# Seven pairs of converted weight blocks and three raw buffers in place of six and four

## The chip, the cores and the metric

The kernel runs on one core of one Trainium2 chip. The metric is the device time of one execution in microseconds (us); the median of the runs shown counts.

## The reference

One sequence of 256 tokens of 1024 features runs through two stacks of two layers each, all in float32. A layer of the first stack is a half-weighted SwiGLU block, a mixer and another half-weighted SwiGLU block:

```
x = x + 0.5 * swiglu(rms_norm(x, norm_ffn1[l]), ...)      # d_ff 2816
x = x + hybrid_mixer(rms_norm(x, norm_mix[l]), w_in[l], ...)
x = x + 0.5 * swiglu(rms_norm(x, norm_ffn2[l]), ...)
```

The hybrid mixer has dilated window attention (12 heads in three groups) and stick-breaking attention (4 heads), each behind a sigmoid gate, and a projection out. A layer of the second stack is a mixer with four branches (compressed, selected and window attention; a sliding window attention with sinks; a 31-tap depthwise convolution with a layer norm; windowed mean pooling), each gated by `sigmoid(h @ w_gate)`, followed by a block `w_down(gelu(conv3(h @ w_up_gate)) * conv3(h @ w_up_value))`, each with a norm behind it. A last RMS norm closes the first stack. All weight matrices together are some 366 MB and are read once.

## The kernel before

All activations stay on the chip; only weights stream in. Every weight product is done as three float32r products: both factors are split into a rounded part and the rest (`h` and `l`, or `wh` and `wl`), and `h*wh + h*wl + l*wh` is summed in PSUM (`mm3`, lines 191 to 194, and the two transposed forms `lin_T` and `lin_T2`, lines 202 to 228).

A weight block of 128 partitions x 1024 elements (512 KB; some are smaller) passes four engines in `chunk` (lines 112 to 120). SyncE issues its load into a tile of the pool `rawp` (line 115); ScalarE rounds it into a tile `wh` (line 118); VectorE subtracts, `wl = raw - wh` (line 119); TensorE uses the pair. The pool `wp` has `bufs` tiles of each of the two tags `wh` and `wl`, so `bufs` is the number of converted pairs. A load can be issued when the tile that it overwrites was read for the last time, by the subtraction; a rounding can start when the last matmul has read the pair that it overwrites. Each tile of a full block has 4 KB in each partition.

The loops over the blocks differ in how long they hold a pair. `lin` (line 196) runs all eight k for the first 128 tokens and then for the second, so a pair is given back in the second pass. `lin_T`, `lin_T2` and `kouter` (line 249) use a block up and give it back, except that `kouter` with `late` holds the last four blocks for the second half of the tokens, so that TensorE has work while the norms behind the first half run. In the second mixer (`mixer2`, line 660) some blocks are used up faster: `compress` (line 766) needs eight matmuls of 256 columns for a block, where the others need 12 of 512, and one projection of 280 columns has blocks of 280 KB.

The kernel is one unrolled program of 30596 instructions. Which engine runs what is written in the source; the order on each engine and all semaphores are laid down when the program is built, by a planner that goes by the order in the source, its own estimate of the durations, and the buffers that are free. `behind` (line 277) sets a few orders by hand. Each engine then runs its queue strictly in that order. The convolution of the second mixer (lines 951 to 956) is 120 VectorE instructions per layer that depend on little else; its result is wanted at the end of the mixer. `stat` (line 57) hands out tiles of 8 columns for maxima, sums and norms.

Of the kernel before, what the change touches and what calls it, by code (L numbers as in the profile page):

```python
# [8 lines left out]
F32 = mybir.dt.float32  # L9
F32R = mybir.dt.float32r  # L10
BF16 = mybir.dt.bfloat16
AF = mybir.ActivationFunctionType
OP = mybir.AluOpType
AX = mybir.AxisListType

P = 128
# [9 lines left out]
def body(tc, ctx, I, C, out, upto=99):  # L26
    nc = tc.nc
    V, S, G = nc.vector, nc.scalar, nc.gpsimd

    rawp = ctx.enter_context(tc.tile_pool(name="rawp", bufs=4))  # L30
    wp = ctx.enter_context(tc.tile_pool(name="wp", bufs=6))
    act = ctx.enter_context(tc.tile_pool(name="act", bufs=1))
    gp = ctx.enter_context(tc.tile_pool(name="gp", bufs=1))
    st = ctx.enter_context(tc.tile_pool(name="st", bufs=1))
# [6 lines left out]
    def nm(s):  # L41
        uid[0] += 1
        return f"{s}{uid[0]}"
# [11 lines left out]
        return psum.tile([P, 512], F32, tag="aux", name=nm("aux"))  # L55

    def stat(cols=1):
        return st.tile([P, 8], F32, tag="st", name=nm("st"), bufs=48)[:, :cols]

    pending, pows, early = [], [], []  # L60

# [89 lines left out]

    def split(src, hi, lo, scale=None):
        if scale is None:
            S.activation(hi, src, AF.Copy)
            V.tensor_sub(lo, src, hi.bitcast(F32))  # L155
        else:
            S.activation(hi, src, AF.Copy, scale=scale)  # L157
            V.scalar_tensor_tensor(lo, src, scale, hi.bitcast(F32), op0=OP.mult, op1=OP.subtract)  # L158

    def transposed(srcs):  # L160
        p = aux_ps()
# [13 lines left out]
    def split_T(tag, srcs, scale=None):  # L175

        xt = XT()
        if len(srcs) == 1:
            n = srcs[0].shape[-1]
            b = big(tag, "hl", F32R)  # L180
            hi, lo = b[:, :n], b[:, 512:512 + n]
            split(transposed(blocks(srcs[0], n // P)), hi, lo, scale)
            xt.add(hi, lo, n // P)
        else:
            bh, bl = big(tag, "hi", F32R), big(tag, "lo", F32R)
            for s, hi, lo in zip(srcs, halves(bh), halves(bl)):
                split(transposed(blocks(s)), hi, lo, scale)
                xt.add(hi, lo)
        return xt
# [91 lines left out]
    def square(src):  # L281

        junk = unit("junk", BF16, 1024)[:, :src.shape[-1]]
        m = stat()
        S.activation(junk, src, AF.Square, scale=1.0 / 32.0, accum_out=m)
        return m

    def rstd_of(parts):

        r, r2 = stat(), stat()  # L290
        V.tensor_scalar(r, parts[0], parts[1], EPS, op0=OP.add, op1=OP.add)
        pows.append(G.tensor_tensor(r2, r, half, op=OP.pow))
        return r2
# [24 lines left out]
    class Halves:  # L318
# [5 lines left out]
        def put(self, t, b, src):  # L324
            hi, lo = (halves(x)[b] for x in self.bufs[t])
            split(transposed(blocks(src)), hi, lo, self.scale)
            self.xts[t].add(hi, lo)
# [91 lines left out]
    def attend1(qkn, vs):  # L419
# [3 lines left out]
        for t in range(2):  # L423
# [27 lines left out]
            def scores(js):  # L451

                r = [([], stat(4), stat(4)) for _ in js]
                for gi, gs in enumerate(groups):
                    n = len(gs) * nk * P
                    pss = [aux_ps()[:, :n] for _ in js]
                    for gg in gs:
                        for kt in range(nk):
                            c0 = ((gg - gs[0]) * nk + kt) * P
                            for ps, j in zip(pss, js):  # L460
                                h = gg * 4 + j
                                nc.tensor.matmul(ps[:, c0:c0 + P], qk(h, False, t), qk(h, True, kt),
                                                 start=(gg == gs[0] and kt == 0), stop=(gg == gs[-1] and kt == nk - 1))
                    for ps, (ps_l, mx, sm) in zip(pss, r):
                        e = unit("e")[:, :n]
                        masked(e, ps, dilm[t][:, gs[0]:gs[-1] + 1, :].rearrange("p g k -> p (g k)"), mx[:, gi:gi + 1])
                        ps_l.append(e)
                return r
# [780 lines left out]
```

## Time and profile before

| | |
|---|---|
| median of 3 runs | 2100.12 us (2099.17 to 2103.72) |
| the profiled execution's own time | 2096.72 us |
| its span, first to last instruction | 2094.9 us |
| TensorE matmul busy, share of the span | 98% |
| TensorE weight load busy | 83% |
| VectorE busy | 75% |
| ScalarE busy | 57% |
| mean granted TensorE clock | 0.999 |
| read from HBM | 366.10 MB, 175 GB/s over the span |

The profile is that of one execution. PE is TensorE's matmul, PEld its weight load, DVE VectorE, ACT ScalarE, SP SyncE; a q behind a name is the queue that an engine issues from. A busy time is the union of the records, and matmul records overlap: the records of 512 columns are about 0.39 us long and start 0.23 us apart. Idle time is put down to the work whose end released the waiting instruction.

### The profile page before, as it was taken

How to read it: one execution, taken by the hardware profiler on the slowest of the kernel's cores; microseconds unless marked ns; L12 is line 12 of the kernel's file. 1: busy time of each engine (PE TensorE's matmuls, PEld its weight loads, DVE VectorE, ACT ScalarE, POOL GpSimd, SP SyncE). 2: the span in 40 equal slices, each digit the busy share in tenths (PEclk: the TensorE clock that was granted, in tenths of full speed). 3: DMA queues.
4: the chain of work that ended last, by engine and by line, in shares of the span. 5: the costliest groups of instructions: out<-in, count | busy, mean ns of one | idle time of the engine just before them, and what ended most of it. 6: DMA issues, size and time to landing. Idle time of an engine off the chain costs nothing.

```text
span 2094.9 us, 30596 instructions
## 1 busy us (share of the span) xinstructions
PE 2059.3 (98%) x11428; PEld 1737.9 (83%) x11428; DVE 1574.7 (75%) x2696; ACT 1185.2 (57%) x1905; POOL 27.6 (1%) x51
## 2 busy tenths in 40 slices
PE   8999999999999999999999999999999999999998
PEld 7888877888888887788887877779987877788997
DVE  7865466886688556678757999778867899877883
ACT  6555565554555455565545665456655565557652
POOL 0000000000000000000000000000000000000000
PEclk9999999999999999999999999999999999999999
DMA  9665535666666654466666733556665744365653
GB/s 268 194 191 173 191 120 165 187 190 192 181 191 190 186 177 150 142 176 188 191 190 183 229 121 121 175 164 194 183 193 176 219 149 142 101 202 172 181 189 112
DMA packets 248102, 368.70 MB, mean 176 GB/s; under 512 B 14608, under 2 KB 123536, under 8 KB 247952
## 3 DMA queue, kind: packets, MB, share of 16 engines
q1 hardware_dynamic: 247088, 366.17, 57.1%
q8 instruction: 90, 1.47, 0.3%
q0 software_dynamic: 576, 0.46, 0.1%
q14 instruction: 60, 0.49, 0.1%
q10 hardware_dynamic: 288, 0.11, 0.0%
HBM read 366.10 MB, written 1.05 MB: 175 GB/s over the span
## 4 chain that ended last, share of the span: by engine, by line
PE 87%; DVE 7%; ACT 2%; DMA 2%; issue 1%; POOL 0%; DVEq 0%; POOLq 0%; SPq 0%; ACTq 0%
PE lin L194 16%; PE lin L193 16%; PE lin L192 15%; PE lin L226 15%; PE lin L227 8%; PE lin L214 3%; PE lin L213 3%; PE lin L212 3%; PE aux L163 3%; DVE wl L119 2%; DVE cy L955 1%; ACT wh L118 1%; DVE e L275 1%; PE aux L650 1%; PE aux L597 1%
## 5 line engine op out<-in xcount | busy, mean ns | idle before, releaser
L119 DVE TENSOR_TENSOR wl<-raw,wh 128x1024 fp32r<-128x1024 f32 (+2 forms) x689 | 834.9, 1216 | 377.1 <-ACT wh L118 370.6
L118 ACT ACTIVATE wh<-raw 128x1024 fp32r<-128x1024 f32 (+2 forms) x689 | 721.9, 1052 | 509.6 <-PE lin L194 273.7
L226 PE MATMUL lin<-x,wh 128*128 128x512 f32 x1408 | 490.5, 394 | 0.0
L227 PE MATMUL lin<-x,wl 128*128 128x256 f32 x1408 | 392.2, 279 | 0.4 <-DVE wl L119 0.4
L194 PE MATMUL lin<-wh,x 128*128 128x512 f32 (+2 forms) x896 | 347.0, 388 | 2.7 <-DVE x L158 2.6
L193 PE MATMUL lin<-wl,x 128*128 128x512 f32 (+2 forms) x896 | 347.5, 388 | 1.9 <-DVE wl L119 1.9
L192 PE MATMUL lin<-wh,x 128*128 128x512 f32 (+2 forms) x896 | 347.4, 388 | 0.8 <-ACT x L157 0.8
L226 PEld LDWEIGHTS lin<-x,wh 128*128 128x128 f32 x1408 | 263.9, 187 | 59.5 <-DVE x L158 0.3
L227 PEld LDWEIGHTS lin<-x,wl 128*128 128x128 f32 x1408 | 265.5, 189 | 1.1 <-DVE wl L119 0.8
L192 PEld LDWEIGHTS lin<-wh,x 128*128 128x128 f32 x896 | 168.4, 188 | 39.4 <-issue 5.2
L194 PEld LDWEIGHTS lin<-wh,x 128*128 128x128 f32 x896 | 168.4, 188 | 38.9 <-DVE x L158 7.3
L193 PEld LDWEIGHTS lin<-wl,x 128*128 128x128 f32 x896 | 168.5, 188 | 35.0 <-DVE wl L119 3.0
L194 PE MATMUL lin<-wh,lo 128*128 128x512 f32 x480 | 188.2, 392 | 0.5 <-DVE lo L155 0.5
L192 PE MATMUL lin<-wh,hi 128*128 128x512 f32 x480 | 187.6, 391 | 0.0
L193 PE MATMUL lin<-wl,hi 128*128 128x512 f32 x480 | 187.0, 390 | 0.0
L213 PE MATMUL lin<-x,wh 128*128 128x256 f32 x576 | 163.2, 283 | 0.0
L214 PE MATMUL lin<-x,wl 128*128 128x256 f32 x576 | 163.0, 283 | 0.0
L212 PE MATMUL lin<-x,wh 128*128 128x256 f32 x576 | 163.0, 283 | 0.0
L213 PEld LDWEIGHTS lin<-x,wh 128*128 128x128 f32 x576 | 110.6, 192 | 0.1
L212 PEld LDWEIGHTS lin<-x,wh 128*128 128x128 f32 x576 | 110.6, 192 | 0.1
L214 PEld LDWEIGHTS lin<-x,wl 128*128 128x128 f32 x576 | 110.6, 192 | 0.0
L194 PEld LDWEIGHTS lin<-wh,lo 128*128 128x128 f32 x480 | 90.1, 188 | 19.6 <-DVE lo L155 1.3
(300 smaller groups left out, 2609.6 us busy)
## 6 DMA issues: line engine op xcount, KB each, us to landing
raw<-in_ffn_w_up_dram SPq DMA_DIRECT2D x168, 512.0 KB, 3.8
raw<-in_ffn_w_down_dram SPq DMA_DIRECT2D x132, 512.0 KB, 3.7
raw<-in_w_in_dram SPq DMA_DIRECT2D x132, 512.0 KB, 4.0
raw<-in_ffn_w_gate_dram SPq DMA_DIRECT2D x87, 512.0 KB, 3.8
raw<-in_w_gate_dram SPq DMA_DIRECT2D x64, 512.0 KB, 4.3
raw<-in_w_branch_dram SPq DMA_DIRECT2D x32, 512.0 KB, 3.5
raw<-in_w_out_dram SPq DMA_DIRECT2D x16, 512.0 KB, 4.5
raw<-in_nsa_cmp_w_dram SPq DMA_DIRECT2D x16, 512.0 KB, 4.4
```

The lines of the kernel that those rows point to most:

```text
L118: S.activation(wh, raw, AF.Copy)
L119: V.tensor_sub(wl, raw, wh.bitcast(F32))
L163: nc.tensor.transpose(p[:, i * P:(i + 1) * P], s, ident)
L192: nc.tensor.matmul(ps, xt.h[k], w[0], start=start, stop=False)
L193: nc.tensor.matmul(ps, xt.h[k], w[1], start=False, stop=False)
L194: nc.tensor.matmul(ps, xt.l[k], w[0], start=False, stop=stop)
L212: nc.tensor.matmul(o, wh, xh, start=k == 0 and i % 2 == 0, stop=False)
L213: nc.tensor.matmul(o, wh, xl, start=False, stop=False)
L214: nc.tensor.matmul(o, wl, xh, start=False, stop=k == 7 and i % 2 == 1)
L226: nc.tensor.matmul(o, wh, x, start=k == 0, stop=False)
L227: nc.tensor.matmul(o[:, :T], wl, x[:, :T], start=False, stop=k == 7)
L275: V.tensor_tensor_reduce(out, ps, mask, 1.0, NEG, OP.add, OP.max, mx)
```

## The change

The pool of raw blocks has three tiles in place of four, the pool of converted blocks seven pairs in place of six. The statistics tiles go from 48 to 40, 256 bytes of each partition less, beside 8 KB more for the pair and 4 KB less for the raw tile. `split` gives back the instructions that it issues; nobody uses them.

```diff
-    rawp = ctx.enter_context(tc.tile_pool(name="rawp", bufs=4))
-    wp = ctx.enter_context(tc.tile_pool(name="wp", bufs=6))
+    rawp = ctx.enter_context(tc.tile_pool(name="rawp", bufs=3))
+    wp = ctx.enter_context(tc.tile_pool(name="wp", bufs=7))
...
-        return st.tile([P, 8], F32, tag="st", name=nm("st"), bufs=48)[:, :cols]
+        return st.tile([P, 8], F32, tag="st", name=nm("st"), bufs=40)[:, :cols]
...
     def split(src, hi, lo, scale=None):
         if scale is None:
-            S.activation(hi, src, AF.Copy)
-            V.tensor_sub(lo, src, hi.bitcast(F32))
-        else:
-            S.activation(hi, src, AF.Copy, scale=scale)
-            V.scalar_tensor_tensor(lo, src, scale, hi.bitcast(F32), op0=OP.mult, op1=OP.subtract)
+            return S.activation(hi, src, AF.Copy), V.tensor_sub(lo, src, hi.bitcast(F32))
+        return (S.activation(hi, src, AF.Copy, scale=scale),
+                V.scalar_tensor_tensor(lo, src, scale, hi.bitcast(F32), op0=OP.mult, op1=OP.subtract))
```

## Rows read from the trace of the kernel before

**Rows 1.** Page, busy time: engine, us, share of the span, instructions.
```profile
PE 2059.3 (98%) x11428; PEld 1737.9 (83%) x11428; DVE 1574.7 (75%) x2696; ACT 1185.2 (57%) x1905; POOL 27.6 (1%) x51
```

**Rows 2.** Table of stages: length; busy us, instructions by engine; clock; DMA share; GB/s.
```profile
20.00:165.00 145.00, 145.00 (x797) 125.96 (x796) 112.43 (x146) 82.57 (x122) 0.00 (x0) 1.00 0.70 214
...
250.00:300.00 50.00, 48.06 (x314) 38.58 (x314) 33.36 (x86) 29.16 (x53) 0.00 (x0) 1.00 0.40 127
...
800.00:850.00 50.00, 47.68 (x318) 37.88 (x316) 36.02 (x95) 32.60 (x62) 0.00 (x0) 1.00 0.34 105
...
1150.00:1330.00 180.00, 175.41 (x1007) 140.46 (x1008) 171.41 (x429) 106.24 (x218) 2.30 (x3) 1.00 0.51 157
1645.00:1830.00 185.00, 179.14 (x1014) 142.73 (x1014) 173.04 (x431) 106.18 (x218) 2.08 (x2) 0.99 0.49 153
```

**Rows 3.** Waits of weight loads: who for whom; total us, times, longest us.
```profile
PEld lin L194 <- DVE x L158: 7.3, 12, 1.1
...
PEld aux L163 <- DVE kd L572: 4.0, 2, 2.3
...
PEld lin L193 <- DVE wl L119: 3.0, 5, 1.0
...
PEld lin L227 <- DVE wl L119: 0.8, 1, 0.8
...
PEld lin L192 <- ACT wh L118: 0.6, 3, 0.2
```

**Rows 4.** Groups by form: line, engine, tiles, count; busy us, mean ns; idle before.
```profile
L119 DVE TENSOR_TENSOR wl<-raw,wh 128x1024 fp32r<-128x1024 f32 x679 | 827.7, 1223 | 373.0 <-ACT wh L118 366.6
L118 ACT ACTIVATE wh<-raw 128x1024 fp32r<-128x1024 f32 x679 | 715.3, 1058 | 503.5 <-PE lin L194 273.7 <-issue 156.9 <-PE lin L213 41.9
```

**Rows 5.** Timelines of ScalarE, VectorE, SyncE near 550 us: start, length, what, idle before.
```profile
549.35 1.06 ACT L118 ACTIVATE wh<-raw 128x1024 fp32r<-128x1024 f32 x1 [1.66 <-PE lin L194]
552.07 1.06 ACT L118 ACTIVATE wh<-raw 128x1024 fp32r<-128x1024 f32 x1 [1.66 <-PE lin L194]
...
550.44 1.23 DVE L119 TENSOR_TENSOR wl<-raw,wh 128x1024 fp32r<-128x1024 f32 x1 [1.50 <-ACT wh L118]
...
551.69 0.37 SPq L115 DMA_DIRECT2D raw<-in_ffn_w_up_dram  x1
```

**Rows 6.** Timelines of TensorE and VectorE in the second mixer's attention.
```profile
1271.36 0.50 PE L192 MATMUL lin<-wh,x 128*128 128x512 f32 x1
...
1272.80 0.50 PE L193 MATMUL lin<-wl,x 128*128 128x512 f32 x1
...
1271.44 1.22 DVE L119 TENSOR_TENSOR wl<-raw,wh 128x1024 fp32r<-128x1024 f32 x1
```

**Rows 7.** DMA issues from 1150 to 1175 us: count, KB each, median us to landing.
```profile
raw<-in_w_in_dram SPq DMA_DIRECT2D x7, 512.0 KB, 4.3
raw<-in_w_in_dram SPq DMA_DIRECT2D x4, 280.0 KB, 3.2
```

**Rows 8.** SyncE's timeline; line 118 from 1144 to 1186 us (ns min/median/max; idle until).
```profile
1157.65 18.02 SPq L115 DMA_DIRECT2D raw<-in_w_in_dram  x12
...
L118 ACT ACTIVATE wh<-raw x21: 672/1057/1065, 1144.5 to 1184.7; 128x1024 fp32r<-128x1024 f32 x17, 128x560 fp32r<-128x560 f32 x4
...
  DMA raw<-in_w_in_dram: 3.4, 6
```

**Rows 9.** Timelines of SyncE and VectorE at the start.
```profile
13.58 2.23 SPq L115 DMA_DIRECT2D raw<-in_ffn_w_gate_dram  x2
...
14.18 1.22 DVE L119 TENSOR_TENSOR wl<-raw,wh 128x1024 fp32r<-128x1024 f32 x1
```

**Rows 10.** Table of stages, the 5 us in which the granted clock fell.
```profile
1820.00:1825.00 5.00, 4.10 (x22) 3.45 (x22) 1.77 (x3) 1.06 (x1) 1.56 (x1) 0.81 0.25 57
```

## The prediction

> **What bounds the kernel now.** I read the busy times of the engines first: TensorE is busy for 2059.3 us of a span of 2094.9 us, so at most 35.6 us of the span can be won by feeding it better [rows 1]. VectorE has 75% over the whole. The table of stages then says where the idle time lies. In long stretches of plain weight products TensorE is busy for all of it (145.00 of 145 us from 20 to 165 us), and there no buffer can help. It idles in the first mixer's attention (1.94 us from 250 to 300 us, 2.32 us in the second layer's counterpart) and in the two passes of the second mixer (4.6 of 180 us and 5.9 of 185 us). In those two passes VectorE is busy for 171.4 of 180 and 173.0 of 185 us, so there are two nearly full engines that wait for each other [rows 2].
>
> The Trainium skill (Perfetto Trace Analysis, Identifying the Most-Contended Engine) says that busy matmuls are a poor measure of headroom and that the busy share of the weight loads is a good one. Weight loads are busy for 83% here, so by that rule 17% of the span, some 357 us, would be open. In the stretch in which TensorE never waits the weight loads have 125.96 of 145 us, 87%, so this trace doesn't bear the rule out: 83% is close to full [rows 1, 2].
>
> The third view is what the weight loads waited for. Waits for a converted block are small: 3.0 us for wl before line 193, 0.8 us for wl before line 227, 0.6 us for wh before line 192, 4.4 us in nine places of the whole run. Waits for the two rows that head the list, activations being turned (7.3 us) and a rope result (4.0 us), have nothing to do with the weights [rows 3].
>
> **The weight pipeline.** A block of 512 KB is loaded by SyncE into a raw buffer, ScalarE rounds it to wh in 1.06 us, VectorE takes the difference to wl in 1.22 us; 679 full blocks [rows 4]. In a steady stretch wh starts every 2.72 us, each time after ScalarE waited 1.6 us for a matmul to give back a pair; the load that follows is issued when wl is done, the difference that ends at 551.67 us being followed by a load at 551.69 us [rows 5]. So in the steady state the six pairs are full, four raw blocks wait landed behind them, and TensorE sets the pace.
>
> **The change, part by part.**
>
> *One pair more.* No instruction is added. In the steady state each block is converted one release, 2.72 us, earlier, and TensorE gains nothing, for it never waits there. What can go are waits for wl and wh: of the 4.4 us the 0.8 us of line 227 belongs to the first blocks, where no pair is short, which leaves 3.6 us. The longest of them is about 1 us, shorter than the 2.72 us of lead, so each would go if nothing took its place. But they lie in the passes in which VectorE has 95% and 94% [rows 2, 3]. There an earlier difference is another VectorE instruction later. An example: at 1271.36 TensorE starts one weight product, and the next starts only at 1272.80, right behind a difference that VectorE ran from 1271.44 to 1272.66 [rows 6]. With a pair more this difference would have been done before; what VectorE does in its place is a step of the rope that ends 1.2 us earlier, or one of the convolution. Bounds: 0 if all is given back, 3.6 us if nothing is; half, 1.8 us, because one of the two neighbours is filler (the convolution) and the other is a chain.
>
> *One raw buffer less.* The load of block n+3, not n+4, now waits for the difference of block n. A raw buffer's round is 4.3 us to land, 1.06 and 1.22 us to convert, 6.6 us; four buffers deliver a block every 1.65 us, three one every 2.2 us [rows 4, 7]. The steady use is 2.72 us a block, so three still keep up, with 19% to spare in place of 39%. They don't in the middle of the second mixer, where blocks are small or serve few columns: there 12 loads are issued in 18.02 us, 1.50 us each, and ScalarE already waits 3.4 us for raw data, in six places [rows 8]. A 280 KB block's round there is 3.2 us to land, 0.67 us for wh (the shortest of that line) and in the same proportion 0.77 us for wl, 4.6 us, or 1.55 us a block with three buffers [rows 7, 8]. Four such and eight full blocks take 4 x 1.55 + 8 x 2.2 = 23.8 us, 5.8 us more than now; the extra pair holds one block, worth 2.72 us of TensorE, so up to 3.1 us a layer can reach TensorE, 6.2 us in the two. The lower end is zero: VectorE has independent convolution steps to put in the holes, and TensorE waits for the rope in that stage in any case (4.0 us in the run [rows 3]). I take 0.5 us a layer, 1.0 us, close to the lower end, because ScalarE's present 3.4 us a layer of waiting for raw data stand against only 3.0 us in the whole run that weight loads waited for wl [rows 3, 8].
>
> *The start.* With four buffers the first load after the constants goes at 13.58 us; with three the buffer that it wants is released by the difference that ends at 15.40 us (14.18 + 1.22), 1.8 us later [rows 9]. From 20 us on TensorE is always busy [rows 2], and the store fills while it works on the blocks already in. Bounds 0 and 1.8 us; I take 0.3 us, since a block is used in 2.72 us and loads still come faster.
>
> *The rest.* Eight small statistics tiles fewer (40 in place of 48): each mixer makes a few dozen, and a tile comes free long before forty others were made; cost nothing, and if one were short it would be the planner's order that moves, which stands below. split() returns what it issued, in the same order: nothing. The longer order of SyncE's queue matters only where a small load stands behind a waiting weight load: the norm gains, the pooling matrix and the inverse counts wait behind loads that may now go 1 to 2 us later; all of them are issued ahead of need except the counts.
>
> *The order of work.* The order of each engine's instructions is planned when the program is built, and free buffers are part of the plan. Six pairs or seven is another plan in every stage with dependent chains. No row shows it. The nearest rows are the two chain waits that now cost most, 7.3 and 4.0 us [rows 3]; moving half of either way is 5 us, to both sides, and I take zero.
>
> The sum: -1.8 + 1.0 + 0.3 = -0.5 us. The profiled execution took 2096.72 us, 1.8 us beyond its span and 3.4 us below the median of 2100.12 us; minus 0.5 us it is 2096.2 us, and on the median's footing **2099.6 us**.
>
> **The rivals.** *Filler for the chains* (faster). If a pair more lets TensorE run a whole block of weight products, 2.72 us, inside every attention burst in which it now stands idle, then half of the idle time of the two second-mixer passes and the two attentions of the first, (4.6 + 5.9 + 1.9 + 2.3) / 2 = 7.3 us, goes: 2092.8 us. For it speaks that the converted block came last in rows 6; against it that only 4.4 us in the run is put down to converted blocks, and that VectorE is nearly full there. The Trainium skill (Perfetto Trace Analysis, Optimization Strategy) says that a gap that repeats on the engine that should be full can mean too few buffers for the next tile; this trace has such a gap in the two passes, and none in the plain stretches.
>
> *Three raw buffers are too few* (slower). The price is the 6.2 us worked out above, at the burst of each second mixer: 2106.3 us. It decides from the point at which a raw round exceeds three times what TensorE needs for a block, 8.2 us in the steady state (6.6 us now, so landing would have to rise from 4.3 to 5.9 us), and 4.5 us (3 x 1.50) in the burst, where it is exceeded already. For it speaks that loads land in 4.3 us there; against it that ScalarE's present waits there hardly reach TensorE.
>
> *The plan moves against it or for it.* The 5 us of the plan's order either way: 2095 or 2105 us.
>
> *The granted clock.* In the 5 us from 1820 us the mean granted clock is 0.81, so TensorE ran for part of them at 1.2 instead of 2.4 GHz, in a stretch in which it was idle for 0.9 us [rows 10]; over the second pass this leaves 0.99, and the first pass kept 1.00 [rows 2]. 1% of 185 us is 1.9 us, which may go, or come in the first pass too. It widens the range and is no case.
>
> *The rule of the weight loads' share* would put the gain in the tens of us; 1%.
>
> **How the numbers follow.** Nothing within 0.2% (4.2 us, about what can be told from no change here), that is 2095.9 to 2104.3 us: 0.51. Faster: 0.19 for filler, 0.07 for the plan, 0.01 for the rule, 0.27. Slower: 0.14 for the raw buffers, 0.08 for the plan, 0.22. The range reaches from below the filler's time with a clock that holds (2092.8 - 1.9, and a little for the half that I left out) to the raw rival's with a fall more (2106.3 + 1.9): 2090 to 2108 us.
>
> **What would show it.** The extra pair: ScalarE's wh in the steady stretch still waits for a matmul and still starts every 2.72 us; waits of weight loads for wl fall from 3.8 us to under 2 us. The raw buffer: ScalarE's waits for raw data grow from 3.4 us in the burst, and the 12 loads take over 20 us. The start: no new TensorE wait after 20 us. Wrong would be: TensorE waiting for wl in plain stretches, idle time of the two passes changed by more than 4 us, or VectorE's share there falling under 90%.

## The result: slower by 0.6%, and the profile after

| | before | after |
|---|---|---|
| median of 4 runs each, us | 2099.95 | 2113.17 (2109.57 to 2114.36) |
| ratio of times, 95% interval | | 1.0063 (1.0049 to 1.0076) |
| the profiled execution, us | 2096.72 | 2109.57 |
| its span, us | 2094.9 | 2107.8 |

The change costs 13 us. The forecast was 2099.6 us with a range up to 2108, so the range missed it. Measured a second time, further below, the same kernel has a ratio of 1.0042 (1.0029 to 1.0055), so the loss is some 9 to 13 us. The lines of the changed kernel from 155 on stand two lower than in the kernel before: 226 is now 224, 234 is 232, 298 is 296. Lines 118 and 119 stay.

Busy times first: TensorE has 2064.1 us in place of 2059.3 [rows 1], in a span 12.9 us longer. So 8.1 us of the 12.9 are idle time (43.7 us in place of 35.6), and 4.8 us are longer busy time, to which the text comes back below. The table of stages says where the first of the idle time is (columns as in [rows 2]):

```profile
20.00:65.00 45.00, 41.06 (x231) 35.03 (x231) 34.53 (x46) 27.64 (x41) 0.00 (x0) 1.00 0.79 236
65.00:165.00 100.00, 100.00 (x538) 85.82 (x538) 75.33 (x98) 54.45 (x81) 0.00 (x0) 1.00 0.66 193
...
1160.00:1345.00 185.00, 179.84 (x1024) 143.18 (x1023) 175.01 (x432) 110.44 (x221) 1.75 (x3) 1.00 0.52 156
1660.00:1845.00 185.00, 180.09 (x1019) 142.86 (x1018) 175.37 (x434) 108.07 (x218) 1.22 (x2) 1.00 0.52 156
```

In the first SwiGLU block, where TensorE never waited before [rows 2], it now stands for 3.94 of 45 us. The two passes of the second mixer, on which the forecast had put its whole attention, stand for 5.2 and 4.9 us; in the same two stretches of the kernel before it was 4.3 and 5.9 us, together as much. Next the waits (who for whom; total us, times, longest):

```profile
ACT wh L118 <- DMA raw<-in_ffn_w_up_dram: 40.1, 33, 3.2
ACT wh L118 <- DMA raw<-in_w_in_dram: 33.0, 33, 2.5
ACT wh L118 <- DMA raw<-in_w_gate_dram: 26.3, 24, 3.3
ACT wh L118 <- DMA raw<-in_ffn_w_gate_dram: 19.7, 13, 3.6
ACT wh L118 <- DMA raw<-in_ffn_w_down_dram: 13.5, 12, 1.5
...
PEld aux L161 <- DVE x L296: 5.6, 9, 2.2
PEld lin L224 <- DVE su L232: 5.2, 4, 1.9
...
PEld lin L191 <- DVE wl L119: 4.0, 9, 0.9
```

ScalarE's roundings wait for raw data for 132.6 us in the five largest rows; before the five largest were 8.3, 6.1, 3.7, 2.4 and 1.0 us, 21.5 together. The row that is quite new is the second of TensorE's: weight loads of the SwiGLU block wait for `su`, VectorE's sum that reads a PSUM tile and so frees it for the next product. And the wait for wl, which the seventh pair should have taken away, is 4.0 us in nine places in place of 3.0 in five [rows 3].

**How late data stop TensorE.** The timelines of ScalarE, VectorE and TensorE of the changed kernel at the first stall (start, length, what, idle time before):

```profile
22.29 1.06 ACT L118 ACTIVATE wh<-raw 128x1024 fp32r<-128x1024 f32 x1 [3.29 <-DMA raw<-in_ffn_w_gate_dram]
23.25 0.64 ACT L231 ACTIVATE su<-lin 128x256 f32<-128x256 f32 x2
...
23.38 1.23 DVE L119 TENSOR_TENSOR wl<-raw,wh 128x1024 fp32r<-128x1024 f32 x1 [4.00 <-ACT wh L118]
24.52 0.75 DVE L232 TENSOR_TENSOR su<-lin,su 128x256 f32<-128x256 f32 x2
...
23.60 0.28 PE L225 MATMUL lin<-x,wl 128*128 128x256 f32 x1
24.99 0.50 PE L224 MATMUL lin<-x,wh 128*128 128x512 f32 x1 [1.12 <-DVE su L232]
```

and ScalarE of the kernel before at the same place:

```profile
18.75 1.05 ACT L118 ACTIVATE wh<-raw 128x1024 fp32r<-128x1024 f32 x1
20.50 0.73 ACT L233 ACTIVATE su<-lin 128x256 f32<-128x256 f32 x2 [0.70 <-PE lin L227]
```

The sixth rounding and the first sums stand one behind the other in ScalarE's queue in both kernels. Before, the rounding's data were there and the sums ran at 20.50, as soon as their product was done. After, the rounding waits 3.29 us for its load, and the sums, whose product is just as early, run at 23.25 behind it. VectorE's half follows at 24.52, the PSUM tile comes free, and TensorE starts at 24.99. The planner has not put more roundings ahead of the sums: the first four pairs of sums have 6, 8, 10 and 13 roundings ahead of them now, and had 6, 9, 11 and 14 before.

In this first stall the sums are not the whole of it. The product that starts at 24.99 uses the late block itself, whose difference ends at 24.61 (23.38 + 1.23), so with the sums out of the way TensorE could have finished hardly any of it sooner. In the third of the four stalls the sums stand alone:

```profile
47.17 0.28 PE L225 MATMUL lin<-x,wl 128*128 128x256 f32 x1
...
55.44 0.50 PE L224 MATMUL lin<-x,wh 128*128 128x512 f32 x1 [1.59 <-DVE su L232]
...
47.90 1.06 ACT L118 ACTIVATE wh<-raw 128x1024 fp32r<-128x1024 f32 x1 [0.96 <-DMA raw<-in_ffn_w_up_dram]
49.95 1.06 ACT L118 ACTIVATE wh<-raw 128x1024 fp32r<-128x1024 f32 x1 [1.00 <-DMA raw<-in_ffn_w_gate_dram]
...
52.73 1.06 ACT L118 ACTIVATE wh<-raw 128x1024 fp32r<-128x1024 f32 x1 [1.20 <-DMA raw<-in_ffn_w_gate_dram]
53.70 0.64 ACT L231 ACTIVATE su<-lin 128x256 f32<-128x256 f32 x2
...
46.42 1.22 DVE L119 TENSOR_TENSOR wl<-raw,wh 128x1024 fp32r<-128x1024 f32 x1 [0.64 <-ACT wh L118]
...
54.97 0.75 DVE L232 TENSOR_TENSOR su<-lin,su 128x256 f32<-128x256 f32 x2
```

The last matmul of an up product begins at 47.17. Its sums run at 53.70, behind three roundings that waited 0.96, 1.00 and 1.20 us for data. TensorE stands for 1.59 us until VectorE has freed the tile, though the block that it goes on with, counted at eight pairs of matmuls to a block, was converted at 47.64 (46.42 + 1.22).

The same happens on VectorE's queue at the end of a SwiGLU block, where the residual add frees the next norm (ScalarE, VectorE and TensorE near 366 us):

```profile
361.58 1.06 ACT L118 ACTIVATE wh<-raw 128x1024 fp32r<-128x1024 f32 x1 [3.34 <-DMA raw<-in_ffn_w_gate_dram]
365.46 1.06 ACT L118 ACTIVATE wh<-raw 128x1024 fp32r<-128x1024 f32 x1 [2.82 <-DMA raw<-in_ffn_w_up_dram]
...
366.55 1.23 DVE L119 TENSOR_TENSOR wl<-raw,wh 128x1024 fp32r<-128x1024 f32 x1 [1.90 <-ACT wh L118]
367.69 0.68 DVE L296 SCALAR_TENSOR_TENSOR x<-lin,x 128x512 f32<-128x512 f32 x1
...
368.44 0.66 PE L161 MATMUL aux<-ident,x 128*128 128x128 f32 x4 [1.77 <-DVE x L296]
```

A difference that is late because its rounding waited 2.82 us for data runs at 366.55, when the add could have run (the last matmul of its product began at 366.03 and such a one is 0.4 us long); the add comes 1.1 us later and TensorE waits 1.77 us for it.

### The profile page after: what moved, and what is told of

Same layout as the page of the kernel before. It is cut to its first block, busy times and chain, and to the rows that moved or that the text cites. A ratio compares the mean times of both kernels' runs of the same rounds, so it can differ in the third digit from the quotient of the medians.

```text
span 2107.8 us, 30577 instructions
## 1 busy us (share of the span) xinstructions
PE 2064.1 (98%) x11428; PEld 1739.3 (83%) x11428; DVE 1574.6 (75%) x2696; ACT 1193.7 (57%) x1905; POOL 26.2 (1%) x51
## 4 chain that ended last, share of the span: by engine, by line
PE 80%; DVE 8%; DMA 6%; ACT 3%; issue 2%; POOL 0%; SPq 0%; DVEq 0%; ACTq 0%; POOLq 0%
PE lin L192 14%; PE lin L191 14%; PE lin L190 14%; PE lin L224 14%; PE lin L225 7%; PE lin L212 3%; PE lin L210 3%; PE lin L211 3%; DVE wl L119 3%; PE aux L161 3%; ACT wh L118 2%; DVE cy L953 1%; DMA raw<-in_ffn_w_up_dram 1%; DMA raw<-in_w_in_dram 1%; DMA raw<-in_w_gate_dram 1%
## 5 line engine op out<-in xcount | busy, mean ns | idle before, releaser
L190 PEld LDWEIGHTS lin<-wh,hi 128*128 128x128 f32 x480 | 90.1, 188 | 18.4
```

The lines of the kernel that those rows point to most:

```text
L190: nc.tensor.matmul(ps, xt.h[k], w[0], start=start, stop=False)
```

## The experiments

Three theories to begin with. RAW: three raw buffers let roundings wait for data at the head of in-order queues, with work behind them that TensorE needs. PAIR: the seventh pair lets the planner put roundings ahead of other work, with any number of raw buffers. PLAN: any other buffer count gives another order, with losses and gains that have no pattern. The "14 us" of the expectations are the two largest rows of raw waits of the kernel before. Ratios are to the kernel before on the same chip, with 95% intervals.

**Three raw buffers alone.**

```diff
-    rawp = ctx.enter_context(tc.tile_pool(name="rawp", bufs=4))
+    rawp = ctx.enter_context(tc.tile_pool(name="rawp", bufs=3))
```

> Three raw buffers, six pairs, nothing else changed. Theory RAW (three raw buffers let ScalarE's roundings stand waiting for data at the head of its queue, with the sums that free PSUM behind them): the whole loss of the change comes with this part alone, 2113 us (2109 to 2118), ScalarE's roundings wait for raw data over 80 us in the run (14 us before), and TensorE stands for some 4 to 6 us in the first SwiGLU block between 20 and 65 us behind VectorE's sums of line 234. Theory PAIR (the seventh pair lets the planner place roundings ahead of other work, and would with any number of raw buffers): within 3 us of before, 2097 to 2103 us, no such stall. Theory PLAN (any other buffer count gives another order, some us to either side, with no pattern): anywhere from 2095 to 2113 us, with the loss in other places than in the changed kernel.

Measured: 2112.79 us, 1.0062 (1.0047 to 1.0077). A stretch of its table of stages, and one of its waits:

```profile
20.00:65.00 45.00, 40.89 (x229) 34.62 (x228) 33.82 (x46) 26.91 (x41) 0.00 (x0) 1.00 0.74 229
```

```profile
PEld lin L226 <- DVE su L234: 5.4, 4, 1.6
```

The whole loss, with the same stall of 4.1 us at the same place. PAIR falls. The roundings' waits for raw data are over 80 us as expected: the six largest rows are 31.9, 22.1, 15.1, 14.0, 13.6 and 11.2 us.

**Seven pairs with four raw buffers, and its control.** Room for the pair is made with 16 activation tiles of the SwiGLU blocks in place of 18.

```diff
-    wp = ctx.enter_context(tc.tile_pool(name="wp", bufs=6))
+    wp = ctx.enter_context(tc.tile_pool(name="wp", bufs=7))
...
-        return act.tile([P, cols], dt, tag="u", name=nm(name), bufs=18)
+        return act.tile([P, cols], dt, tag="u", name=nm(name), bufs=16)
...
-        return st.tile([P, 8], F32, tag="st", name=nm("st"), bufs=48)[:, :cols]
+        return st.tile([P, 8], F32, tag="st", name=nm("st"), bufs=40)[:, :cols]
```

> Seven pairs and four raw buffers. The 4 KB that this needs in each partition are taken from the pool of the SwiGLU blocks' activations (16 tiles in place of 18), statistics tiles 40. To be read against the kernel with 16 such tiles, four raw buffers and six pairs. Theory RAW: no loss by the pair, within 3 us of that control, ScalarE waits for raw data about as before (under 30 us), no stall between 20 and 65 us. Theory PAIR: 8 us or more slower than the control, with the stalls behind the sums in the first SwiGLU block. The gain forecast for the pair was 1.8 us at most half given back: 1 to 4 us under the control if it is there.

The control has the line of the 16 tiles alone:

> Control: before with 16 in place of 18 activation tiles of the SwiGLU blocks, raw buffers and pairs unchanged. No theory says anything of it except PLAN (up to 5 us either way). Otherwise 2100 us, or some us more if a tile is short at the seams of two SwiGLU blocks; ScalarE's wait for raw data near 14 us.

Measured: seven pairs 2097.91 us, 0.9979 (0.9970 to 0.9988); control 2099.60 us, 0.9992 (0.9980 to 1.0005). In the control each engine's instructions stand in the same order as in the kernel before, so the 16 activation tiles have no part in the difference. The 40 statistics tiles have no control of their own; the three runs with four or five raw buffers that have 40 of them are not slower than the kernel before. The pair alone is worth 0.21% against the kernel before (4 us) and 0.13% against the control (3 us, or 2 by the medians), and from the control alone the intervals would not tell it. The profiles agree that it is there: TensorE's idle time is 31.3 us with seven pairs (a span of 2097.1 less 2065.8 busy), 35.6 in the kernel before and 37.4 in the control. Stages of the kernel with seven pairs, and the one wait of weight loads for wl that its table has left:

```profile
20.00:65.00 45.00, 45.00 (x257) 38.92 (x256) 39.55 (x54) 30.61 (x47) 0.00 (x0) 1.00 0.88 272
...
1150.00:1335.00 185.00, 181.05 (x1027) 144.10 (x1027) 174.00 (x429) 111.93 (x223) 1.38 (x3) 1.00 0.49 156
1650.00:1835.00 185.00, 181.51 (x1029) 144.38 (x1029) 176.81 (x435) 108.20 (x219) 1.22 (x2) 1.00 0.50 157
```

```profile
PEld lin L225 <- DVE wl L119: 0.8, 1, 0.8
```

No stall at the start, and the five waits for wl of the second mixer [rows 3] are gone, as the forecast had it for the pair. With three raw buffers the times show no gain of the pair, 1.0063 and 1.0042 with seven pairs and 1.0062 with six, but their intervals would hide one of 0.2%. The rows show none for its own waits: TensorE waits for wl in the second mixer for 4.0 us in nine places with seven pairs, and for 4.0 us in eight with six.

**Five raw buffers, six pairs.**

```diff
-    rawp = ctx.enter_context(tc.tile_pool(name="rawp", bufs=4))
+    rawp = ctx.enter_context(tc.tile_pool(name="rawp", bufs=5))
...
-        return st.tile([P, 8], F32, tag="st", name=nm("st"), bufs=48)[:, :cols]
+        return st.tile([P, 8], F32, tag="st", name=nm("st"), bufs=40)[:, :cols]
```

> One raw buffer more than before, six pairs, statistics tiles 40 to make room. Theory RAW: ScalarE's wait for raw data falls below the 14 us of before; since those 14 us hardly held TensorE up, the time is 2100 us or up to 4 us less (2096 to 2101). Theory PAIR: no difference, 2100 us. Theory PLAN: up to 5 us either way.

Measured: 2099.09 us, 0.9994 (0.9983 to 1.0005); the largest raw wait is 8.0 us and the next 3.0. No difference, so four is enough: the step is between four and three. PLAN has nothing to explain here either, though TensorE and VectorE run the second mixer in an order that differs from before.

**Two raw buffers, seven pairs.**

```diff
-    rawp = ctx.enter_context(tc.tile_pool(name="rawp", bufs=4))
-    wp = ctx.enter_context(tc.tile_pool(name="wp", bufs=6))
+    rawp = ctx.enter_context(tc.tile_pool(name="rawp", bufs=2))
+    wp = ctx.enter_context(tc.tile_pool(name="wp", bufs=7))
```

> Two raw buffers, seven pairs (statistics tiles 48). Tests the size of a raw buffer's round and where its shortage begins to decide everywhere. If the round stays what the traces show with three and four buffers (6.6 to 7.1 us from a load's issue to the end of its difference), two buffers give a block every 3.3 to 3.55 us, over the 2.72 us of the steady use, and the run is bound by loads throughout: 689 blocks x 3.3 to 3.55 us = 2274 to 2446 us, and the forecast is 2280 to 2450 us, with TensorE waiting for wh and wl in the plain stretches. Rival: a load lands sooner when fewer are under way (the 4.3 us are mostly time behind other loads); if it lands in 3 us, a block comes every 2.6 us and the time is 2120 to 2160 us.

Measured: 2324.89 us, 1.105 (1.103 to 1.107). SyncE's loads in the plain stretch of the second layer, and what a load took to land from 575 to 640 us:

```profile
620.29 4.16 SPq L115 DMA_DIRECT2D raw<-in_ffn_w_gate_dram  x2
626.42 4.27 SPq L115 DMA_DIRECT2D raw<-in_ffn_w_up_dram  x2
632.76 4.20 SPq L115 DMA_DIRECT2D raw<-in_ffn_w_gate_dram  x2
```

```profile
DMA to landing us min/median/max: 3.5/3.8/4.6
```

Two blocks every 6.13 and 6.34 us, 3.1 to 3.2 us a block: slower than the 2.72 us that TensorE needs, and now loads set the pace in this plain stretch. The time lies in the expected 2280 to 2450 us, but in part by luck: the blocks come faster than the 3.3 to 3.55 us that were expected, 689 of them at 3.1 to 3.2 us would take 2136 to 2205 us, and where the rest goes was not followed. The round is shorter than 6.6 us because a load lands in 3.8 us here. It takes 3.8 us in the same stretch of the kernel before too; there a load is issued every 2.8 us, so no more than two are under way in either kernel, and this stretch says nothing of the rival. From 20 to 60 us, where the kernel before has two to four loads under way, they land in 4.8 us (median), in the changed kernel in 4.6, with two buffers in 3.8. So loads did land sooner there with fewer under way, though not in the rival's 3 us. The steady rule of the forecast (round against buffers times use) holds. With three buffers it leaves 2.1 us a block in the steady state, and indeed TensorE doesn't wait there: 100.00 of 100 us from 65 to 165 us in the changed kernel.

**Sums ahead of roundings by hand.** If TensorE stands because the sums wait behind a rounding in the queue (HEAD OF LINE) and not for want of blocks (SUPPLY), another order must free it, with the same three buffers.

```diff
-                pg = lin_T2(xts, kchunks(wg, c0, 256, 4), blks)
-                pu = lin_T2(xts, kchunks(wu, c0, 256, 4), blks)
+                with behind(sg):
+                    cg = kchunks(wg, c0, 256, 4)
+                pg = lin_T2(xts, cg, blks)
+                with behind(su):
+                    cu = kchunks(wu, c0, 256, 4)
+                pu = lin_T2(xts, cu, blks)
...
+            sg = last_sum[-1]
...
+            su = last_sum[-1]
```

> The changed kernel (three raw buffers, seven pairs) with one order more, set by hand: in a SwiGLU block of the first stack the roundings for the gate and up blocks of a step stand behind the sums of the step before in ScalarE's queue. Theory HEAD OF LINE (TensorE stands because the sums that free its PSUM wait behind a rounding that waits for raw data): the stalls between 20 and 65 us, 4 us of idle TensorE in the changed kernel, fall under 1.5 us, and the time is some 5 us under the changed kernel, 2108 us (2105 to 2111). Theory SUPPLY (blocks simply come too late with three raw buffers, in whatever order): the idle time there stays 3 us or more, and TensorE now waits for wh or wl instead of the sums; 2113 us (2111 to 2116).

> Control for the same order by hand: the kernel before (four raw buffers, six pairs) with it. HEAD OF LINE and SUPPLY both expect nothing, since before has no stall between 20 and 65 us: within 3 us of before, 2098 to 2104 us. If it gains 4 us or more, the order helps by itself, and the run of the changed kernel with it says nothing of the raw buffers.

Measured: on the changed kernel 2124.79 us, 1.0098 (1.0084 to 1.0112); on the kernel before 2102.87 us, 0.9995 (0.9985 to 1.0004). The start and three waits of the changed kernel with the order:

```profile
20.00:65.00 45.00, 44.24 (x255) 38.65 (x254) 35.35 (x51) 26.88 (x43) 0.00 (x0) 1.00 0.74 222
```

```profile
ACT wh L118 <- DMA raw<-in_ffn_w_down_dram: 83.6, 80, 2.6
...
PEld aux L161 <- DVE x L296: 10.4, 7, 3.1
PE aux L161 <- DVE x L296: 7.6, 5, 2.7
```

Half of this was expected. The stalls at the start go as HEAD OF LINE said, from 3.94 to 0.76 us, and the waits for `su` are gone: for three of the four stalls blocks were there. The 0.76 us that stay are one wait for wl at 25 us, of the block that came late in the first stall; so much is SUPPLY. But the total is worse, by 0.35 to 0.56% of the time (1.0098 against 1.0063 and 1.0042). The roundings now run ahead less in every SwiGLU block of the first stack, those of the down product wait for data (83.6 us; 13.5 in the changed kernel), and the victim is the residual add at the seam: TensorE waits 10.4 us for it, against 5.6 in the changed kernel and 2.7 in the kernel before. With four raw buffers the same order costs nothing: that wait is 2.1 us there, the one of the down product's roundings 14.4 us. So it is the order and the shortage together.

**The same order at the start alone.** In the first block of the run, its first six steps or its first three, with the changed kernel itself beside it. Against the kernel with the order everywhere:

```diff
-            sg = last_sum[-1]
+            sg = last_sum[-1] if len(last_sum) <= 24 else None
...
-            su = last_sum[-1]
+            su = last_sum[-1] if len(last_sum) <= 24 else None
```

> The changed kernel once more, unaltered, as the yardstick for the other two of this call and for one question of its own: in the first SwiGLU blocks pairs of matmuls (512 and 256 columns) came 346.7 or 353.3 ns apart in the profiles so far, one of the two over a whole stage; in the first profile of the changed kernel the stages from 65 to 165 us and from 575 to 715 us had 353 ns, the one from 410 to 520 us 347 ns. If this belongs to the program, the same stages have 353 ns again; if it is drawn anew in each execution, other stages have it. Time: 2113 us (2110 to 2116); stall of some 4 us between 20 and 65 us as before.

> The changed kernel with sums ahead of roundings by hand in the first SwiGLU block of the run alone (its first six steps), all else in the planner's order. Theory HEAD OF LINE: the idle time between 20 and 65 us falls from 3.9 to some 0.8 us, as in the kernel with that order everywhere, nothing is lost in the later blocks, whose order is not touched, and the time is 3 us under the changed kernel (1 to 5). Rival REPAID: what the sums gain the roundings lose, fewer blocks are in store when the down product begins, and the 3 us come back as a stall before 300 us, within 1 us of the changed kernel or slower.

> The same in the first three steps alone, so that from the fourth on roundings may again run as far ahead as buffers let them. HEAD OF LINE: the stalls at 25 and 48 us of the changed kernel are shortened, the later ones stay in part: idle time between 20 and 65 us 1 to 3 us, time 1 to 3 us under the changed kernel. REPAID: no difference to the changed kernel.

Measured: changed kernel 2111.71 us, 1.0042 (1.0029 to 1.0055); six steps 2108.59 us, 1.0017 (1.0007 to 1.0028); three steps (`<= 12`) 2111.15 us, 1.0033 (1.0021 to 1.0046). From 20 to 65 us, one after the other in this order:

```profile
20.00:65.00 45.00, 40.82 (x230) 34.69 (x229) 33.65 (x45) 27.05 (x40) 0.00 (x0) 1.00 0.79 235
```

```profile
20.00:65.00 45.00, 44.23 (x254) 38.54 (x253) 35.30 (x50) 26.71 (x43) 0.00 (x0) 1.00 0.74 219
```

```profile
20.00:65.00 45.00, 44.61 (x257) 39.02 (x256) 36.48 (x50) 28.16 (x42) 0.00 (x0) 1.00 0.78 232
```

With six steps the 4.2 us of idle time fall to 0.8. The ratio falls by 0.25%, 5 us, with intervals that just don't meet; the medians lie 3.1 us apart. Expected were 1 to 5 us. The profiles show where the saving lasts: idle time of TensorE up to 1150 us and in the first pass of the second mixer, for the changed kernel and then for the one with six steps:

```profile
0.00:1150.00 1150.00, 1131.22 (x5994) 948.89 (x5995) 788.60 (x1204) 644.29 (x1005) 12.72 (x30) 1.00 0.60 180
1150.00:1345.00 195.00, 189.53 (x1065) 150.61 (x1065) 178.82 (x434) 114.69 (x225) 1.75 (x3) 1.00 0.53 158
```

```profile
0.00:1150.00 1150.00, 1134.94 (x6026) 952.94 (x6027) 791.60 (x1207) 646.79 (x1008) 12.72 (x30) 1.00 0.61 182
1150.00:1345.00 195.00, 188.64 (x1059) 150.17 (x1058) 181.27 (x440) 114.68 (x226) 1.75 (x3) 0.99 0.51 151
```

Up to 1150 us it is 18.8 against 15.1 us, so REPAID, a stall before 300 us, falls. In the two passes of the second mixer this one execution loses nearly as much again, 43.7 and 43.6 us over the whole spans; its granted clock fell in both passes, where the changed kernel's did not, and from 113 us on every engine has the same instructions in the same order in both kernels, so this is a difference between two executions and its cause stays open. That the saving lasts to the end of the run rests on the times of the 9 and 12 runs. Three steps free the start as well, up to 65 us, but 1.5 us of waits for the sums come between 75 and 83 us. The time falls by 0.09%, inside what its interval allows for no gain at all; that one is not settled. So of the loss of the change 3 to 5 us are shown to be the sums behind late roundings in the first block.

**Five raw buffers and seven pairs**, 14 activation tiles and 40 statistics tiles:

```diff
-    rawp = ctx.enter_context(tc.tile_pool(name="rawp", bufs=4))
-    wp = ctx.enter_context(tc.tile_pool(name="wp", bufs=6))
+    rawp = ctx.enter_context(tc.tile_pool(name="rawp", bufs=5))
+    wp = ctx.enter_context(tc.tile_pool(name="wp", bufs=7))
...
-        return act.tile([P, cols], dt, tag="u", name=nm(name), bufs=18)
+        return act.tile([P, cols], dt, tag="u", name=nm(name), bufs=14)
```

> Five raw buffers and seven pairs, 14 activation tiles in the SwiGLU blocks, 40 statistics tiles. Raw buffers beyond four brought nothing with six pairs, the seventh pair with four brought some 3 to 4 us. If the two are independent: 2097 to 2099 us, as with four and seven. If the seventh pair is worth more the more is landed behind it: 2092 to 2096 us.

Measured: 2096.86 us, 0.9966 (0.9953 to 0.9978), 7 us faster than the kernel before on the same chip. Whether it beats four and seven (0.9979) the intervals don't say, so neither of the two expectations is settled. The room for the pair was in the activation tiles, not in the raw ones.

## Why the prediction was wrong

**What bounds the kernel** was right: TensorE is full in plain stretches, and a buffer helps or hurts only where other work hangs on it. One reading was not: "four raw blocks wait landed behind them". A load is issued every 2.72 us and lands 3.8 us later there, so of the four blocks one is being converted, one or two are still under way and one or two wait.

**One pair more**, -1.8 us between 0 and -3.6: sign and mechanism right, at the upper end of its size. With four raw buffers it brought 3 to 4 us and took the five waits for wl away. In the change no gain of it is to be seen: the waits for wl rose from 3.8 us to 4.8 (4.0 and 0.8), where the text wanted them under 2. The forecast added the two parts as if they were independent. They stand in series, a pair being filled from a raw block; that late raw blocks are what kept the seventh pair from helping is read from these rows and not shown by a run.

The Trainium skill (Perfetto Trace Analysis, Optimization Strategy) says that a gap that repeats on the engine that should be full can mean too few buffers for the next tile. The runs agree with it for the pairs once raw blocks are at hand: in the second mixer, from 1150 to 1335 and from 1650 to 1835 us, TensorE's idle time is 3.9 and 3.5 us with seven pairs and four raw buffers, 4.6 and 5.9 us with six.

**One raw buffer less**, +1.0 us between 0 and 6.2: this is the step that failed, together with the start. Alone it measures 13 us (1.0062). The burst in the second mixer went as worked out: the forecast gave its twelve loads 23.8 us, SyncE needed 23.91 us (18.02 before [rows 8]):

```profile
1170.43 23.91 SPq L115 DMA_DIRECT2D raw<-in_w_in_dram  x12
```

It hardly reached TensorE: idle time in the two passes is 5.2 and 4.9 us, 4.3 and 5.9 before, where the text took half a us for each. What was overlooked lay elsewhere: "three still keep up, with 19% to spare" was read as "no cost in plain stretches". The mean rate does keep up. But a late block costs more than its own lateness: ScalarE and VectorE ran their instructions in the order laid down, and a rounding that waited for data held the sums behind it (those of the product whose last matmul began at 47.17 us ran at 53.70) and a late difference the residual add (1.1 us). The size of this term had been judged by the rows of a kernel with four buffers, in which such a wait did not reach TensorE.

**The start**, 0.3 us between 0 and 1.8: it cost 5 us of the 13 (the product that started at 59.5 us before starts at 64.9). The later first load was right, 15.58 us where the text said 15.40. But the upper bound took a load that goes 1.8 us later to land 1.8 us later. The load that was issued at 13.58 before, and those issued from 15 to 19 us after, in this order:

```profile
DMA to landing us min/median/max: 3.9/3.9/3.9
```

```profile
DMA to landing us min/median/max: 6.5/6.7/6.8
```

So the block lands at 22.26 in place of 17.43 us, 4.8 us later. In the kernel before the loads issued from 15 to 19 us take 6.3 to 6.6 us as well; constants are loaded beside them in both, and no run took these away. The step "from 20 us on the store fills while it works" was wrong too: after these, loads in the first block land in 4.6 us, not 4.3, and the store is empty, so each rounding waits for its load, with sums behind it. The "new TensorE wait after 20 us" that the text named as the sign of a wrong step is what came.

**The rivals.** "Three raw buffers are too few" had the right cause and the wrong place, 2106.3 us in place of 2113. Its point of decision, a round of 8.2 us, was not reached (a block issued at 33.86 us was converted at 40.96, a round of 7.1 us), and it decided all the same. The point is right for the steady state alone, as two buffers show. "Filler" was not seen with three buffers. "The plan either way" at 5 us was not needed. "The rest" (statistics tiles, `split`) was nothing, as far as the runs tell: the loss is whole without it (three raw buffers alone), and the run with four raw buffers that has both is not slower.

**Where the 12.9 us between the two profiled spans are.** Counted up to the same matmul of the run in both (11428 in each), TensorE's idle time in the changed kernel is 3.9 us ahead of the kernel before after the first 65 us; 5.7 up to 380 us, behind the seam of the add of 367.69; 6.8 behind the next layer's seam near 915 us; 6.9 behind the first pass of the second mixer, 8.5 ahead of its second pass, 7.5 behind that, and 8.1 at the end. The other 4.8 us are busy time. Of these 1.3 us from 65 to 165 us and 2.0 us from 575 to 715 us are no effect of the change but the spacing of matmuls told of below; 1.6 us go the other way, which the kernel before lost in its fall of the clock [rows 10] and the changed kernel didn't; the rest was not followed. That late blocks are behind the idle time past the first block is read from rows; no run took those places away one by one.

## What to carry to other kernels

A buffer's count is not judged by its mean rate alone: look at what stands behind the instruction that waits for it, on an engine that runs its queue in order, and who waits for that. When a stall is put down to work behind a late block, see whether the next product needs the late block itself: then another order wins little. Before giving a stage's buffers away, look where the pipeline starts empty (the first block, the seam after a chain); there the slack that the steady state shows doesn't exist. An order by hand can move such a stall to the next victim while the shortage itself stays.

## What the runs showed of the hardware that was not expected

In the first stack's SwiGLU blocks the pairs of a 512 and a 256 column matmul come 346.7 or 353.3 ns apart, at a granted clock of 1.00 either way, and one of the two holds for a whole stage in nearly all cases. It differs between executions of one program: the changed kernel has 353 ns from 65 to 165 us in one profile and 347 in the other, and the other way round from 410 to 520 us. The group of 512 columns from 65 to 165 us, first and second profile of the same kernel (ns min/median/max):

```profile
L224 PE MATMUL lin<-x,wh x216: 395/398/403, 64.9 to 140.9; 128*128 128x512 f32 x108
```

```profile
L224 PE MATMUL lin<-x,wh x218: 391/391/391, 64.7 to 139.9; 128*128 128x512 f32 x109
```

Each stage in the slow spacing costs 1.3 to 2.2 us, some 6 us in a run (the profile of five raw buffers and seven pairs has it in most stages and still spans 2096.0 us). The kernel before had none of it in its profile, which is near the fastest of all its runs; the control with 16 activation tiles, the same instructions in the same order, has it from 65 to 165 us (median 398 ns), so it does not come with the change. Two profiles of this kernel can thus differ by some 6 us with no change in the code, and a difference between two of them is read by idle time and by the same matmul's start, not by the span. What sets the spacing stays open.
